# Down projections of a hybrid encoder's gated MLPs, computed on 2x2 blocks by Strassen's algorithm

## The chip, the core and the metric

The kernel runs on one core of a Trainium2 chip. The metric is the device time of one execution in microseconds (us), lower is better. The median of three executions of the kernel before is 1244.37 us (1243.29 to 1244.93).

## The reference, cut to what matters

Everything is float32. Two layers stand one behind the other: a state space mixer (S5) and a differential attention, and behind each a gated MLP, which is what the change touches:

```
def conv_ffn(h, w_up, conv_w, conv_b, w_down):    # h: 512 tokens x 1024; w_up: 1024 x 5632; w_down: 2816 x 1024
    u = h @ w_up
    u = depthwise_conv3_over_tokens(u, conv_w) + conv_b
    g, val = jnp.split(u, 2, axis=-1)             # gate and value, 2816 channels each
    return (jax.nn.silu(g) * val) @ w_down

for i in range(2):
    h = h + mixer_i(rmsnorm(h, norm_mix_g[i]))
    h = h + conv_ffn(rmsnorm(h, norm_ffn_g[i]), ...)
return rmsnorm(h, final_norm_g)
```

## The kernel before, in words

**Split operands.** A product in nearly full float32 precision is made of three faster matmuls. Each operand is split into a high part (ScalarE copies it, rounded, to the type fp32r) and a low part (the value less its high part, one subtraction on VectorE), and `mm3` (lines 801 to 804) adds up high*high, high*low and low*high in PSUM. So each weight and each activation costs one ScalarE and one VectorE instruction per split before TensorE can use it.

**Weights** come as a stream of units (`WStream`, lines 112 to 152): each unit is loaded into one of two raw buffers and split in two halves into one of two pairs of hi and lo buffers. A unit of an up projection (`wup`) has 2048 columns: 8 tiles of 128 input channels by 128 outputs for the gate, and 8 for the value. A unit of a down projection (`wdn`) has 1408: 11 tiles of 128 hidden channels for one tile of 128 outputs.

**The MLP** (`ffn`, lines 909 to 1088) keeps the 512 tokens along the free dimension. The hidden channels are 22 tiles, `j`. Phase by phase: `up(0)` to `up(11)`, `down(0)` over tiles 0 to 10, `up(12)` to `up(21)`, `down(1)` over tiles 11 to 21. An up phase makes, for each `j`, a gate and a value in PSUM (24 matmuls of 512 columns each; "half slot" below). `evac` multiplies them by the norm's factor (`tpb`, VectorE, L927) and starts the convolution (`acc`, ScalarE, L929); half a slot later `conv` adds the other two taps on VectorE (L934, L935), takes silu, multiplies gate by value (L944) and splits the result into `act` (L945 on ScalarE, L946 on VectorE). `later` and `flush` put these a half slot behind. A down phase makes 8 output tiles `m` of 33 matmuls each, and VectorE adds each to the residual `h` (L1005). In the second down phase each finished tile goes through `norm_part`: high part and square on ScalarE, low part on VectorE (L821), the sum of squares on GpSimd (L829). In the last layer six tiles go that way and `finish` makes the last two in halves of 256 tokens.

**What sets the order.** Nothing is scheduled by a planner: every engine executes its instructions in the order in which the program writes them, and waits on semaphores. The matmuls are written ahead of the VectorE and ScalarE work that stands behind them.

Of the kernel before, what the change touches and what calls it, by code (L numbers as in the profile page):

```python
# [9 lines left out]
F32 = mybir.dt.float32  # L10
# [27 lines left out]
def trunk(ctx, tc, xs, xt, sp, bx, cx, sv, vec, lamv, biasw, wglu, wup, wdn, wv, wqk, wo, out):  # L38
# [72 lines left out]

    class WStream:
# [11 lines left out]

        def split(self, half, parts="hl", eng=V):

            i = self.ns
            if i >= len(units):
                return
            n = units[i][1]  # L130
            if half == 0 and "h" in parts:
                self.hl[i] = (
                    self.whl.tile([128, 2048], F32R, tag="hi", name=f"hi{i}"),
                    self.whl.tile([128, 2048], F32R, tag="lo", name=f"lo{i}"),
                )
            h0, h1 = (0, n // 256 * 128) if half == 0 else (n // 256 * 128, n)
            hi, lo = self.hl[i]
            if "h" in parts:
                S.activation(hi[:, h0:h1], self.raw[i][:, h0:h1], AF.Copy)  # L139
            if "l" in parts:  # L140
                eng.tensor_tensor(lo[:, h0:h1], self.raw[i][:, h0:h1], hi[:, h0:h1].bitcast(F32), op=ALU.subtract)  # L141
                if half == 1:
                    del self.raw[i]
                    self.ns += 1

        def start(self):
            self.cur += 1
            while self.nd < min(self.cur + 3, len(units)):
                self.dma()
            return self.hl.pop(self.cur)  # L150

    ws = WStream()
# [571 lines left out]
    ws.whl = pool("whl", 2, "right")  # L724
# [71 lines left out]
    xhi = xnp.tile([128, 8, 512], F32R, name="xhi")  # L796
# [18 lines left out]
    def norm_part(m, gcol, first, split=True):  # L815

        settle()
        if split:
            gc = vect[:, gcol + m:gcol + m + 1]
            S.activation(xhi[:, m], h[:, m], AF.Copy, scale=gc)  # L820
            pend.append(lambda: V.scalar_tensor_tensor(  # L821
                xlo[:, m], h[:, m], gc, xhi[:, m].bitcast(F32), op0=ALU.mult, op1=ALU.subtract))
# [86 lines left out]
    def ffn(l, next_gcol):  # L909
        fp = pool(f"ffn{l}", 1, "left")  # L910
        tpb = [fp.tile([128, 514], F32, name=f"tpb{i}") for i in range(4)]
# [3 lines left out]
        acts = {}  # L915
        state = {"rb": None, "slot": None, "nt": 0}
# [4 lines left out]
        def evac(j, gv, ps):  # L921
            tb = tpb[state["nt"] % 4]
# [5 lines left out]
            acc = fp.tile([128, 512], F32, tag="acc", name="acc", bufs=4)  # L928
# [4 lines left out]
        def conv(j, gv, tb, cw, acc):  # L933
# [7 lines left out]
            if j % 4 == 0:  # L941
                state["slot"] = arena(F32R, [128, 4, 2, 512], f"act{l}_{j}")
            hi, lo = (state["slot"][:, j % 4, i] for i in range(2))
            V.tensor_tensor(a0, a0, acc, op=ALU.mult)  # L944
            S.activation(hi, a0, AF.Copy)  # L945
            later.append(lambda: V.tensor_tensor(lo, a0, hi.bitcast(F32), op=ALU.subtract))  # L946
            acts[j] = (hi, lo)
# [11 lines left out]
        def up(j):  # L959
            w = ws.start()  # L960
            if j == 0:
# [15 lines left out]
                return  # L977
            for gv in range(2):
                ws.split(gv, "h")
                ps = psd[0].tile([128, 512], F32, tag="mm", name="ps", bufs=6)  # L980
                for k in range(8):
                    upmm(w, gv, k, ps)
                    if j == 1 and gv == 0 and k == 5:
# [4 lines left out]
                        evac(0, 1, pss[1])  # L988
                evac(j, gv, ps)
                if j > 1 or gv == 1:  # L990
                    ws.split(gv, "l")

        def down(hf):
            flush()
            for m in range(8 if hf == 0 or l == 0 else 6):
                wh, wl = ws.start()
                if m == 0:
                    flush()
                ws.split(0)
                ws.split(1)  # L1000
                ps = psd[0].tile([128, 512], F32, tag="mm", name="ps", bufs=6)
# [4 lines left out]
                if hf == 1 and l == 0:  # L1006
                    norm_part(m, next_gcol, m == 0)
                elif hf == 1:
                    norm_part(m, next_gcol, m == 0, False)
                    S.activation(hg[:, m], h[:, m], AF.Copy, scale=vect[:, next_gcol + m:next_gcol + m + 1])  # L1010

        def finish():
# [36 lines left out]
            for c in range(2):  # L1049
                cs = slice(256 * c, 256 * c + 256)  # L1050
                for m in (6, 7):
# [7 lines left out]
                    ps = psd[0].tile([128, 512], F32, tag="mm", name="ps", bufs=6)[:, 0:256]  # L1059
                    for k in range(11):  # L1060
                        ah, al = acts[11 + k]
                        mm3(ps, wh[:, k * 128:k * 128 + 128], wl[:, k * 128:k * 128 + 128], ah[:, cs], al[:, cs],
                            k == 0, k == 10)
# [6 lines left out]
                    V.tensor_tensor(h[:, m, cs], ps, h[:, m, cs], op=ALU.add)  # L1070
# [11 lines left out]
        for j in range(12, 22):  # L1082
            up(j)
        down(1)
# [16 lines left out]
    for eh in range(2):  # L1101
        vps = [bank(t, "vps") for t in (("sc", "sc", "sc", "tr"), ("pj", "pj", "pv", "sc"))[eh]]
        for un in range(4):
            wh, wl = ws.start()
            ws.split(0)
            ws.split(1)
            for kl in range(2):
# [289 lines left out]
    fin = pool("fin", 1, "left")  # L1397
    hg = fin.tile([128, 8, 512], F32, name="hg")
# [4 lines left out]
    fin.release()  # L1403
# [108 lines left out]
```

## Time and profile before

| | |
|---|---|
| median of three runs | 1244.37 us |
| the profiled execution | 1244.6 us, its span 1242.8 us |
| TensorE busy | 1178.8 us, 95% of the span |
| VectorE, ScalarE, GpSimd busy | 826.7, 583.3, 253.1 us |
| up phases | 226 to 346, 408 to 520, 873 to 993, 1055 to 1168 us |
| down phases | 346 to 408, 520 to 582, 993 to 1055, 1168 to 1231 us |
| granted TensorE clock, mean | 0.982 |

The span is the time from the first to the last instruction; the execution has 1.8 us around it. An engine's queue works in order, so an instruction that waits holds up all behind it. "Idle before" in a row is the time in which the engine waited ahead of that instruction, and the arrow names what it waited for. Each matmul shows in the rows with a duration that overlaps the next one's; the pace is the distance from start to start.

### The profile page before, as it was taken

Reading aid. Unit: us, or ns where it says so; the run is one execution under the profiler, and the core shown is the slowest. Engines: PE = TensorE matmul, PEld = TensorE weight load, DVE = VectorE, ACT = ScalarE, POOL = GpSimd, SP = SyncE. Lnnn points to the kernel's source line nnn. Section 1 sums busy time; section 2 is a strip of 40 time slices with the busy share of each in tenths; the row PEclk is TensorE's granted clock in tenths of the full one; section 3 lists DMA queues with packets and bytes.
Section 4 is the critical chain, followed back from the end, with each engine's and each line's share of the span. In section 5 each row is a group of like instructions: output and inputs, shape, how many; then the busy total and the mean of one; then the engine's idle time right before and its main releaser. Section 6 shows DMA issues by size and latency. Waiting matters only on the chain.

```text
span 1242.8 us, 16640 instructions
## 1 busy us (share of the span) xinstructions
PE 1178.8 (95%) x6402; PEld 931.5 (75%) x6402; DVE 826.7 (67%) x1654; ACT 583.3 (47%) x1008; POOL 253.1 (20%) x271
## 2 busy tenths in 40 slices
PE   3885999999999999999998999999999999999996
PEld 1663688888878888788876777678888878888786
DVE  8999876667653466745349899977767643566634
ACT  6774654444432344433247777655444421344431
POOL 3999434000000000011033435423000000000011
PEclk8997999999999999999999999999999999999998
DMA  5005322122223222132332323221222233222222
GB/s 219 2 2 136 137 74 102 68 102 102 80 96 114 68 102 102 70 114 71 90 118 83 90 75 104 72 77 63 97 77 94 81 117 125 68 97 75 92 94 68
DMA packets 23391, 112.32 MB, mean 90 GB/s; under 512 B 2704, under 2 KB 5392, under 8 KB 16144
## 3 DMA queue, kind: packets, MB, share of 16 engines
q1 hardware_dynamic: 21472, 108.64, 25.8%
q0 software_dynamic: 1280, 2.10, 0.9%
q8 instruction: 50, 0.82, 0.3%
q10 hardware_dynamic: 560, 0.52, 0.1%
q14 instruction: 29, 0.24, 0.1%
HBM read 102.86 MB, written 2.10 MB: 84 GB/s over the span
## 4 chain that ended last, share of the span: by engine, by line
PE 83%; DVE 13%; ACT 2%; issue 1%; DMA 0%; SPq 0%; DVEq 0%; ACTq 0%
PE ps L803 20%; PE ps L802 20%; PE ps L804 20%; DVE scn L690 2%; PE pj L802 2%; PE pj L804 2%; PE pj L803 2%; DVE St L696 1%; DVE acc L693 1%; PE po L802 1%; PE po L803 1%; PE po L804 1%; PE vps L1112 1%; DVE qkt L1165 1%; PE vps L1114 1%; PE vps L1113 1%
## 5 line engine op out<-in xcount | busy, mean ns | idle before, releaser
L802 PE MATMUL ps<-xhi,hi 128*128 128x512 f32 x672 | 266.9, 397 | 0.0
L803 PE MATMUL ps<-xlo,hi 128*128 128x512 f32 x672 | 265.7, 395 | 0.0
L804 PE MATMUL ps<-xhi,lo 128*128 128x512 f32 x672 | 264.1, 393 | 0.0
L139 ACT ACTIVATE hi<-raw 128x1024 fp32r<-128x1024 f32 (+2 forms) x216 | 184.2, 874 | 113.5 <-PE ps L803 85.8
L141 DVE TENSOR_TENSOR lo<-raw,hi 128x1024 fp32r<-128x1024 f32 (+3 forms) x178 | 188.2, 1076 | 43.5 <-ACT hi L139 41.8
L927 DVE TENSOR_TENSOR tpb<-ps,rb 128x512 f32<-128x512 f32 x88 | 60.8, 692 | 149.9 <-PE ps L804 144.7
L929 ACT ACTIVATE acc<-tpb,vect 128x512 f32<-128x512 f32 x88 | 71.6, 815 | 168.1 <-DVE tpb L927 168.1
L804 PEld LDWEIGHTS ps<-xhi,lo 128*128 128x128 f32 x672 | 126.1, 188 | 31.7
L802 PEld LDWEIGHTS ps<-xhi,hi 128*128 128x128 f32 x672 | 126.2, 188 | 30.7
L803 PEld LDWEIGHTS ps<-xlo,hi 128*128 128x128 f32 x672 | 126.1, 188 | 29.2
L803 PE MATMUL ps<-act,hi 128*128 128x512 f32 (+1 forms) x374 | 144.2, 385 | 0.2
L802 PE MATMUL ps<-act,hi 128*128 128x512 f32 (+1 forms) x374 | 142.8, 382 | 0.0
L804 PE MATMUL ps<-act,lo 128*128 128x512 f32 (+1 forms) x374 | 142.0, 380 | 0.0
L827 POOL COPY ssum<-sqt 128x512 f32<-128x512 f32 x4 | 2.5, 627 | 656.1 <-ACT sqt L824 656.1
L1005 DVE TENSOR_TENSOR h<-ps,h 128x512 f32<-128x512 f32 x30 | 20.7, 690 | 107.4 <-PE ps L804 107.4
L141 POOL TENSOR_TENSOR lo<-raw,hi 128x512 fp32r<-128x512 f32 (+1 forms) x38 | 61.2, 1615 | 119.9 <-ACT hi L139 119.7
L802 PEld LDWEIGHTS ps<-act,hi 128*128 128x128 f32 x374 | 70.3, 188 | 15.9
L804 PEld LDWEIGHTS ps<-act,lo 128*128 128x128 f32 x374 | 70.2, 188 | 15.7 <-DVE lo L141 1.4
L803 PEld LDWEIGHTS ps<-act,hi 128*128 128x128 f32 x374 | 70.3, 188 | 15.3 <-DVE act L946 1.1
L935 DVE SCALAR_TENSOR_TENSOR acc<-tpb,vect,acc 128x512 f32<-128x512 f32 x88 | 66.2, 752 | 3.1
L934 DVE SCALAR_TENSOR_TENSOR acc<-tpb,vect,acc 128x512 f32<-128x512 f32 x88 | 65.4, 743 | 0.6 <-ACT acc L929 0.6
L945 ACT ACTIVATE act<-acc 128x512 fp32r<-128x512 f32 x44 | 27.8, 633 | 66.2 <-DVE acc L944 66.2
(262 smaller groups left out, 2043.5 us busy)
## 6 DMA issues: line engine op xcount, KB each, us to landing
raw<-wup SPq DMA_DIRECT2D x44, 1024.0 KB, 4.8
raw<-wdn SPq DMA_DIRECT2D x32, 704.0 KB, 4.0
raw<-wqk SPq DMA_DIRECT2D x16, 512.0 KB, 3.5
raw<-wglu SPq DMA_DIRECT2D x4, 1024.0 KB, 4.8
raw<-wv SPq DMA_DIRECT2D x8, 512.0 KB, 3.5
raw<-wo SPq DMA_DIRECT2D x4, 1024.0 KB, 4.8
bias<-biasw SPq DMA_DIRECT2D x8, 448.0 KB, 4.1
cxt<-cx SPq DMA_DIRECT2D x1, 2064.0 KB, 15.8
```

Of the source, the lines that this page charges most:

```text
L139: S.activation(hi[:, h0:h1], self.raw[i][:, h0:h1], AF.Copy)
L141: eng.tensor_tensor(lo[:, h0:h1], self.raw[i][:, h0:h1], hi[:, h0:h1].bitcast(F32), op=ALU.subtract)
L690: V.tensor_tensor(prd[dr], st[:, dr].unsqueeze(1).to_broadcast([128, 2, 2, 32]), cft[dr], op=ALU.mult)
L802: PE.matmul(ps, lhsT=wh, rhs=xh, start=first, stop=False)
L803: PE.matmul(ps, lhsT=wh, rhs=xl, start=False, stop=False)
L804: PE.matmul(ps, lhsT=wl, rhs=xh, start=False, stop=last)
L927: V.tensor_tensor(tb[:, 1:513], ps, state["rb"], op=ALU.mult)
L929: S.activation(acc, tb[:, 1:513], AF.Identity, bias=cb, scale=cw[1])
L934: V.scalar_tensor_tensor(acc, tb[:, 0:512], cw[0], acc, op0=ALU.mult, op1=ALU.add)
L935: V.scalar_tensor_tensor(acc, tb[:, 2:514], cw[2], acc, op0=ALU.mult, op1=ALU.add)
L945: S.activation(hi, a0, AF.Copy)
L1005: V.tensor_tensor(h[:, m], ps, h[:, m], op=ALU.add)
```

## The change

Three things change.

**The down projection.** Output tiles are taken in pairs (m, m+1), hidden tiles in five pairs, tokens in two halves of 256. Each is a 2x2 block product, which Strassen's algorithm (Winograd's form, with 7 products and shared sums) computes with 7 block products instead of 8. A block product is 5 hidden pairs of 3 matmuls with 256 columns. The eleventh hidden tile is left over and multiplied as before, in halves. The four sums of weight blocks are made by VectorE (`Pair.total`) ahead of the splits, in the unused part of the raw buffer. VectorE adds six results out of PSUM for each pair (`add`). The weight buffers become 4 pairs of 1024 columns, and the next load is issued right behind the last split of a raw buffer.

**The operands of the tokens.** Seven blocks of 256 tokens for each hidden pair are made in the up phase (`Acts`): `first` splits one block, `second` makes four sums of blocks and splits six. The first three weight operands of a down phase are made within the up slot before it (`early`).

**The norm's low parts** of tiles 2 to 7 at the end of layer 0's MLP are put off into the attention's value projection (`xlows`). `tpb` and `acc` have three buffers instead of four, and `hg` takes the place of `xhi`.

```diff
+    class Pair:                              # the weight operands of two output tiles
+        def total(self, n):
+            w = self.view                    # w(r, odd): raw unit r, even or odd hidden tiles, 5 x 128; w(1): unused part
+            if n == 2:
+                V.tensor_tensor(w(1), w(1, 0), w(1, 1), op=ALU.add)
+            elif n == 3:
+                V.tensor_tensor(w(1), w(1), w(0, 0), op=ALU.subtract)
+            elif n == 4:
+                V.tensor_tensor(w(0, 1), w(0, 1), w(1), op=ALU.subtract)
+            else:
+                self.x = self.ws.xtile()[:, 0:640].rearrange("p (k c) -> p k c", c=128)
+                V.tensor_tensor(self.x, w(0, 0), w(1, 0), op=ALU.subtract)
...
+            S.activation(hi[:, 0:640]..., self.src(n), AF.Copy)                             # h(n)
...
+            V.tensor_tensor(lo[:, 0:640]..., self.src(n), hi[:, 0:640]..., op=ALU.subtract) # l(n)
...
+            def second(self, pa):                                                           # Acts
+                x = ws.xtile().rearrange("p (n c) -> p n c", c=256)
+                b = pa.rearrange("p j (n c) -> p j n c", c=256)
+                S.activation(self.hl[:, 0, 1:3], b[:, 1], AF.Copy)
+                V.tensor_tensor(x[:, 0], b[:, 0, 1], b[:, 0, 0], op=ALU.subtract)
+                V.tensor_tensor(x[:, 1], b[:, 1, 1], b[:, 0, 1], op=ALU.subtract)
+                V.tensor_tensor(x[:, 2], x[:, 1], b[:, 0, 0], op=ALU.add)
+                V.tensor_tensor(x[:, 3], b[:, 1, 0], x[:, 2], op=ALU.subtract)
+                S.activation(self.hl[:, 0, 3:7], x, AF.Copy)
+                V.tensor_tensor(self.hl[:, 1, 1:3], b[:, 1], self.hl[:, 0, 1:3].bitcast(F32), op=ALU.subtract)
+                later.append(lambda: V.tensor_tensor(self.hl[:, 1, 3:7], x, self.hl[:, 0, 3:7].bitcast(F32),
+                                                     op=ALU.subtract))
...
+                if early and gv == 0:                                                       # up
+                    ws.split(0, "l")
+                    ws.split(1)
+                elif early:
+                    w = ws.hl[ws.cur + 1]
+                    w.total(2)
+                    w.h(2)
+                    w.l(2)
+                    w.total(3)
                 evac(j, gv, ps)
...
         def down(hf):
-            flush()
-            for m in range(8 if hf == 0 or l == 0 else 6):
...
-                for k in range(11):
-                    ah, al = acts[hf * 11 + k]
-                    mm3(ps, wh[:, k * 128:k * 128 + 128], wl[:, k * 128:k * 128 + 128], ah, al, k == 0, k == 10)
-                V.tensor_tensor(h[:, m], ps, h[:, m], op=ALU.add)
...
+                def prod(n, op, name, part=0, first=False):
...
+                    for kp in range(5):
+                        mm2(bank[name][:, half[part]], hi[:, 128 * kp:128 * kp + 128], lo[:, 128 * kp:128 * kp + 128],
+                            *acts[hf, kp].op(op), first and kp == 0)
...
+                prod(0, 0, "b1", 0, True)
+                if prev:
+                    prev()                   # last add of the pair before, and its norm
+                if mp > 0:
+                    w.l(2)
+                    w.total(3)
+                w.h(3)
+                flush()
+                prod(1, 1, "b2", 0, True)
+                add(h[:, m, half[0]], bank["b1"][:, half[0]])
+                w.total(4)
+                w.h(4)
+                w.l(3)
+                prod(2, 3, "b5", 0, True)
+                w.h(5)
+                w.l(4)
+                w.total(6)
+                w.done(0)                    # frees a raw buffer: the next load is issued
+                flush()
+                prod(3, 5, "b1")
+                add(h[:, m:m + 2, half[1]], twice(bank["b5"][:, half[0]]))
+                w.h(6)
+                w.l(5)
+                w.done(1)
+                prod(4, 2, "b2", 1)
+                left(4, "b2")
+                add(h[:, m, half[1]], bank["b1"][:, half[0]])
+                w.l(6)
+                ws.split(0, "h")
+                flush()
+                prod(5, 6, "b4", 0, True)
+                left(5, "b4")
+                add(h[:, m], bank["b2"])
+                norm(m)
+                ws.split(0, "l")
+                ws.split(1, "h")
+                prod(6, 4, "b1")
+                add(h[:, m + 1], bank["b4"])
+                ws.split(1, "l")             # and total(2), h(2) of the next pair
```

On VectorE, where the first up phase ends and the first down phase begins, there stood before (L946 is a low part of `act`, L1005 the first output tile's addition to `h`):

```order
L946 TENSOR_TENSOR act_8_3295<-acc,act_8_3295 128x512
L934 SCALAR_TENSOR_TENSOR acc<-tpb_2585,vect,acc 128x512
L935 SCALAR_TENSOR_TENSOR acc<-tpb_2585,vect,acc 128x512
L141 TENSOR_TENSOR lo_3408<-raw_3333,hi_3407 128x768
L934 SCALAR_TENSOR_TENSOR acc<-tpb_2586,vect,acc 128x512
L935 SCALAR_TENSOR_TENSOR acc<-tpb_2586,vect,acc 128x512
L944 TENSOR_TENSOR acc<-acc 128x512
L946 TENSOR_TENSOR act_8_3295<-acc,act_8_3295 128x512
L141 TENSOR_TENSOR lo_3485<-raw_3405,hi_3484 128x640
L141 TENSOR_TENSOR lo_3485<-raw_3405,hi_3484 128x768
L1005 TENSOR_TENSOR h<-ps,h 128x512
```

At the same place now (L156 and L158 are the weight sums 3 and 4, L174 a weight's low part, L1026 and L1027 the taps of the convolution, L1178 an addition to `h`; the last row is the low part of weight operand 3):

```order
L174 TENSOR_TENSOR lo<-raw_3476,hi 128x640
L156 TENSOR_TENSOR raw_3476<-raw_3476,raw_3396 128x640
L1019 TENSOR_TENSOR tpb_2597<-ps,rb 128x512
L1039 TENSOR_TENSOR act_0_1_2918<-acc,act_0_0_2761 128x512
L1026 SCALAR_TENSOR_TENSOR acc<-tpb_2596,vect,acc 128x512
L1027 SCALAR_TENSOR_TENSOR acc<-tpb_2596,vect,acc 128x512
L1026 SCALAR_TENSOR_TENSOR acc<-tpb_2597,vect,acc 128x512
L1027 SCALAR_TENSOR_TENSOR acc<-tpb_2597,vect,acc 128x512
L1046 TENSOR_TENSOR pa<-acc 128x512
L1178 TENSOR_TENSOR h<-ps,h 128x256
L158 TENSOR_TENSOR raw_3396<-raw_3396,raw_3476 128x5x128
L174 TENSOR_TENSOR lo<-raw_3476,hi 128x640
```

The weight sums and splits now stand between and behind the gate work of the last slot, and the low part that the fourth block product reads is the last row shown.

On TensorE the first output tile of that down phase began before with rows of this kind, eleven hidden tiles of three:

```order
L802 MATMUL ps<-act_0_2718,hi_3407 128x512
L803 MATMUL ps<-act_0_2718,hi_3407 128x512
L804 MATMUL ps<-act_0_2718,lo_3408 128x512
L802 MATMUL ps<-act_0_2718,hi_3407 128x512
L803 MATMUL ps<-act_0_2718,hi_3407 128x512
L804 MATMUL ps<-act_0_2718,lo_3408 128x512
```

And now with a block product of five hidden pairs (`fifth` holds the operands of the fifth pair):

```order
L1150 MATMUL ps<-act_0_0_2761,hi 128x256 x2
L1150 MATMUL ps<-act_0_0_2761,lo 128x256
L1150 MATMUL ps<-act_0_1_2918,hi 128x256 x2
L1150 MATMUL ps<-act_0_1_2918,lo 128x256
L1150 MATMUL ps<-act_0_2_3075,hi 128x256 x2
L1150 MATMUL ps<-act_0_2_3075,lo 128x256
L1150 MATMUL ps<-act_0_3_3232,hi 128x256 x2
L1150 MATMUL ps<-act_0_3_3232,lo 128x256
L1150 MATMUL ps<-fifth,hi 128x256 x2
L1150 MATMUL ps<-fifth,lo 128x256
```

The matmuls are half as wide, and seven such products with twelve left-over matmuls stand where two tiles of 33 stood.

## Rows read from the trace of the kernel before

**Rows 1.** The page: span and busy time by engine (busy us, share, instructions).

```profile
span 1242.8 us, 16640 instructions
PE 1178.8 (95%) x6402; PEld 931.5 (75%) x6402; DVE 826.7 (67%) x1654; ACT 583.3 (47%) x1008; POOL 253.1 (20%) x271
```

**Rows 2.** Busy us (and instructions) by engine in the first up phase and down phase.

```profile
226.00:346.00 120.00, 120.00 (x521) 96.69 (x520) 82.76 (x108) 53.66 (x68) 0.00 (x0) 1.00 0.24 83
...
346.00:408.00 62.00, 62.00 (x266) 49.59 (x265) 24.72 (x33) 14.44 (x20) 0.00 (x0) 1.00 0.36 121
```

**Rows 3.** TensorE's matmuls where 512 columns give way to 256 (start, duration).

```profile
1179.76 0.39 PE L802 MATMUL ps<-act,hi 128*128 128x512 f32 x1
...
1213.36 0.28 PE L802 MATMUL ps<-act,hi 128*128 128x256 f32 x1
...
1219.60 0.28 PE L803 MATMUL ps<-act,hi 128*128 128x256 f32 x1
```

**Rows 4.** VectorE in order of time, from up phase to down phase at 520 us.

```profile
511.45 1.22 DVE L141 TENSOR_TENSOR lo<-raw,hi 128x1024 fp32r<-128x1024 f32 x1
...
519.99 0.69 DVE L927 TENSOR_TENSOR tpb<-ps,rb 128x512 f32<-128x512 f32 x1 [1.93 <-PE ps L804]
520.60 0.68 DVE L946 TENSOR_TENSOR act<-acc,act 128x512 fp32r<-128x512 f32 x1
521.20 0.75 DVE L934 SCALAR_TENSOR_TENSOR acc<-tpb,vect,acc 128x512 f32<-128x512 f32 x1
...
522.65 0.95 DVE L141 TENSOR_TENSOR lo<-raw,hi 128x768 fp32r<-128x768 f32 x1
523.52 0.74 DVE L934 SCALAR_TENSOR_TENSOR acc<-tpb,vect,acc 128x512 f32<-128x512 f32 x1
...
525.15 0.69 DVE L944 TENSOR_TENSOR acc<-acc 128x512 f32<-128x512 f32 x1
...
527.18 1.70 DVE L141 TENSOR_TENSOR lo<-raw,hi 128x640 fp32r<-128x640 f32 x2
528.79 0.68 DVE L1005 TENSOR_TENSOR h<-ps,h 128x512 f32<-128x512 f32 x1
```

**Rows 5.** VectorE, all steps of 256 elements: strided, contiguous, out of PSUM.

```profile
L773 DVE TENSOR_TENSOR gx<-tr,gx 128x256 fp32r<-128x256 f32 x14 | 5.9, 424 | 1.8 <-ACT gx L772 1.4
...
1217.89 0.41 DVE L1070 TENSOR_TENSOR h<-ps,h 128x256 f32<-128x256 f32 x1
...
1228.97 1.74 DVE L1045 TENSOR_TENSOR hg<-hg,rp 128x256 f32<-128x256 f32 x5 [2.22 <-ACT rb L1038]
1230.63 0.47 DVE L1041 SCALAR_TENSOR_TENSOR hg<-h,vect,rp 128x256 f32<-128x256 f32 x1
```

**Rows 6.** ScalarE's high parts and taps; then the loads of `wdn` (KB, us to landing).

```profile
512.11 0.73 ACT L139 ACTIVATE hi<-raw 128x640 fp32r<-128x640 f32 x1
515.12 0.82 ACT L929 ACTIVATE acc<-tpb,vect 128x512 f32<-128x512 f32 x1 [2.29 <-DVE tpb L927]
...
raw<-wdn SPq DMA_DIRECT2D x32, 704.0 KB, 4.0
```

**Rows 7.** TensorE after its longest wait in the attention, then the granted clock there.

```profile
786.51 1.09 PE L1266 MATMUL ptp<-ident,s 128*128 128x128 f32 x4 [2.92 <-DVE s L1256]
...
788.25 0.63 PE L804 MATMUL po<-o,lo 128*128 128x512 f32 x1
788.68 0.63 PE L802 MATMUL po<-o,hi 128*128 128x512 f32 x1
...
788.00:789.00 1.00, 1.00 (x4) 0.81 (x3) 0.86 (x4) 1.00 (x3) 0.00 (x0) 0.50 0.97 410
789.00:790.00 1.00, 1.00 (x5) 0.77 (x5) 1.00 (x2) 1.00 (x3) 0.00 (x0) 0.86 0.89 377
```

**Rows 8.** GpSimd's sum and VectorE's two low parts beside it, second down phase.

```profile
537.88 1.30 POOL L829 TENSOR_TENSOR ssum<-ssum,sqt 128x512 f32<-128x512 f32 x1 [6.39 <-ACT sqt L824]
...
538.39 2.33 DVE L141 TENSOR_TENSOR lo<-raw,hi 128x640 fp32r<-128x640 f32 x2 [1.28 <-ACT hi L139]
```

More of the change, by code (lines that the diff above doesn't have):

```diff
@@ L123, in dma, with tiles @@
                 self.nd += 1
+        def tiles(self):
+            return [self.whl.tile([128, 1024], F32R, tag=t, name=t) for t in ("hi", "lo")]
         def split(self, half, parts="hl", eng=V):
@@ L130, in split @@
             n = units[i][1]
+            pair = i in pair_at
             if half == 0 and "h" in parts:
[L132 to L135, printed above, removed]
+                self.hl[i] = Pair(self, i) if pair else (Cols(), Cols())
+            if pair:
+                for c in parts:
+                    (self.hl[i].h if c == "h" else self.hl[i].l)(half)
+                if half == 1 and "l" in parts:
+                    self.ns += 2
+                return
             h0, h1 = (0, n // 256 * 128) if half == 0 else (n // 256 * 128, n)
@@ L138, in split @@
             if "h" in parts:
+                if half == 0 or n > 1024:
+                    for c, t in zip((hi, lo), self.tiles()):
+                        c.parts.append((t, h0, h1 if n > 1024 else n))
                 S.activation(hi[:, h0:h1], self.raw[i][:, h0:h1], AF.Copy)
@@ L813, in settle, with norm_part @@
         pend.clear()
-    def norm_part(m, gcol, first, split=True):
+    xlows = {}
+    def norm_part(m, gcol, first, split=True, put=None):
         settle()
@@ L909, in ffn @@
     def ffn(l, next_gcol):
+        hg = None
         fp = pool(f"ffn{l}", 1, "left")
-        tpb = [fp.tile([128, 514], F32, name=f"tpb{i}") for i in range(4)]
+        tpb = [fp.tile([128, 514], F32, name=f"tpb{i}") for i in range(3)]
         for t in tpb:
@@ L915, in ffn @@
         acts = {}
+        fifth = [None]
+        ws.xtile = lambda: fp.tile([128, 1024], F32, tag="x", name="x", bufs=1)
         state = {"rb": None, "slot": None, "nt": 0}
@@ L940, in conv @@
             a0 = state["gate"]
[L941 to L947, printed above, removed]
+            hf, jl = j // 11, j % 11
+            if jl == 10:
+                hi, lo = acts[hf, "left"] = [acts[hf, i].rest for i in range(2)]
+                V.tensor_tensor(a0, a0, acc, op=ALU.mult)
+                S.activation(hi, a0, AF.Copy)
+                later.append(lambda: V.tensor_tensor(lo, a0, hi.bitcast(F32), op=ALU.subtract))
+                return
@@ new lines, in conv @@
+            kp = jl // 2
+            if jl % 2 == 0:
+                state["pa"] = fp.tile([128, 2, 512], F32, tag="pa", name="pa", bufs=1)
+                state["pair"] = Acts(hf, kp)
+            pa, ab = state["pa"], state["pair"]
+            V.tensor_tensor(pa[:, jl % 2], a0, acc, op=ALU.mult)
+            wait = hf == 1 and kp == 0
+            if wait and jl % 2 == 1:
+                later.append(lambda: (ab.first(pa), later.append(lambda: ab.second(pa))))
+            elif not wait:
+                later.append(lambda: (ab.first if jl % 2 == 0 else ab.second)(pa))
@@ L977, in up @@
                 return
+            early = ws.ns in pair_at
             for gv in range(2):
-                ws.split(gv, "h")
+                if early and gv == 1:
+                    pass
+                else:
+                    ws.split(gv, "h")
                 ps = psd[0].tile([128, 512], F32, tag="mm", name="ps", bufs=6)
@@ L988, in up, with mm2 @@
                         evac(0, 1, pss[1])
+                if early and gv == 0:
[7 more added lines that the diff above has]
+                    w.total(3)
                 evac(j, gv, ps)
-                if j > 1 or gv == 1:
+                if not early and (j > 1 or gv == 1):
                     ws.split(gv, "l")
+        def mm2(ps, wh, wl, ah, al, first):
+            for i, (w, x) in enumerate(((wh, ah), (wh, al), (wl, ah))):
+                PE.matmul(ps, lhsT=w, rhs=x, start=first and i == 0, stop=True, skip_group_check=True)
@@ L993, in down @@
         def down(hf):
[L994 to L1010 removed]
+            npair = 4 if hf == 0 or l == 0 else 3
```

146 lines of the change are left out of this document (128 added, 18 removed).

## The prediction

> **What bounds the kernel now.** I began with the page: TensorE is busy for 95% of the span, VectorE for 67% [rows 1]. An average over stages says nothing about one stage, so next I read busy time by stretch. In an up phase TensorE is busy for 120.00 of 120.00 us and VectorE for 82.76; in the first down phase TensorE for 62.00 of 62.00 and VectorE for only 24.72 [rows 2]. So the stretches that the change touches are TensorE's, and VectorE has much room in the down phase, less in the up phase. Then I read TensorE's matmuls one by one for their pace, and VectorE's queue in order of time where up turns into down, because the change gives VectorE far more to do just there.
>
> **What TensorE saves.** The pace is read where 512 columns give way to 256 [rows 3]: 144 matmuls from 1179.76 to 1213.36 make 0.2333 us each, 52 from there to 1219.60 make 0.120 each. Half as wide is a little more than half as long. A pair of output tiles was 2 x 33 = 66 matmuls of 512: 15.40 us. It becomes 7 products of 15 matmuls and 12 left-over ones, 117 of 256: 14.04 us. There are 4 + 4 + 4 + 3 = 15 pairs; the last two tiles keep their count. 15 x 1.36 = 20.4 us saved, if nothing waits.
>
> The Trainium skill prices this otherwise ("TensorE: Matmul & The Clock Gate", section Back-to-back issue gap: columns by 2.4 GHz and 2.5 ns more). By that, as an estimate, 216 and 109 ns, so 15 x (14.24 - 12.78) = 21.9 us. The rows differ by 18 and 11 ns a matmul, and I take the rows.
>
> **What VectorE gets, by the piece.** I charge each instruction the distance from its start to the next one's start. From [rows 4]: `tpb` 0.61 (519.99 to 520.60), a low part of 512 elements 0.60, the two taps of a convolution 1.45 (521.20 to 522.65), or 1.63 if the product of gate and value follows (523.52 to 525.15) and with that product 2.24, two low parts of 640 together 1.61 (so 0.80), one of 1024 1.14 (its 1.22 less the same overlap). 256 elements take 0.33 in a row [rows 5], 0.45 if each needs the one before, 0.38 as an `add` out of PSUM. No row shows a sum of 5 x 128 elements at a stride of 256. The nearest is a strided 256 at 424 ns, against 0.41 contiguous [rows 5], so I charge 0.80 as for a plain 640, and 0.85 where the next step needs it. The bounds are half of that and twice it.
>
> **The pairs, once running.** Per pair: seven low parts of 640 (5.6) with two of 128 (0.5), four sums (3.2), four adds of 512 and two of 256 (3.2): 12.5 us beside 14.04 of TensorE. It fits, and I walked through the order for due times. The tightest is weight operand 3: VectorE reaches it some 0.3 us before product 3 needs it. Loads are no limit: a raw buffer is freed 8.6 us before the next pair begins, and a `wdn` load lands after 4.0 [rows 6]. I charge nothing here, and up to 1 us a pair if the sums are dearer.
>
> **The up phase.** Per two hidden tiles, two low parts of 512 (1.2) become low parts of 256, 512 and 1024 and four sums (0.33 + 0.60 + 1.14 + 1.80 = 3.87). The worst half slot is now `tpb` 0.61, sums 1.80, low part 0.60, taps 1.45, weight split 1.14: 5.60. It starts 0.2 after a half slot ends, and what it splits is due 0.47 into the half slot that follows the next 5.6. So it is done at 5.8 and due at 6.07. The half slots beside it need less. No charge; with dearer sums some 0.2 us on 20 such half slots.
>
> **The seam, where up turns into down.** Before, TensorE ran through it without a wait. Now the last up slot of VectorE carries the first three weight operands, and behind it the gate work, and only then comes what product 3 needs. Count from the first matmul of the last up unit; half slots end at 5.6 and 11.2, products are due at 11.2, 13.0, 14.8 and 16.6, and product 3 reads its weight's low part first in its third matmul, at 16.84.
>
> Seam of the first down phase in each layer. VectorE comes free at 5.8, from the worst half slot. Then, in the order of the queue: low parts 0 and 1 (1.60), `tpb` (0.61), a low part of 1024 (1.14), taps and product (2.24), sum 2 (0.85), a wait for ScalarE's high part of it (0.73 by [rows 6] and two hand-overs, 0.83), low part 2 (0.85), sum 3 (0.82), `tpb` (0.61), left-over low part (0.60), taps (1.45), taps and product (2.24), add (0.38), sum 4 (0.85), low part 3 (0.80). That is 15.9, so 21.7 against 16.84: TensorE waits 4.8 us. Behind product 3 stand all other matmuls.
>
> Seam of the second down phase. VectorE comes free of its half slot at 5.05 (`tpb` to 0.8, ScalarE's taps 0.82 [rows 6] and a high part of 256 at about half a 640's, low part 0.38, taps 1.45, split 1.14), and follows with low parts 0 and 1 behind ScalarE (to 6.9), `tpb`, taps and product (9.75), sum 2, wait, low part 2, sum 3 (13.1), `tpb` (13.7), four sums (15.5), low part of 512 (16.1). Product 1 needs that one for its fifth pair at 14.56: 1.5 late. Taps (17.55), low part of 1024 (18.7), which product 2 needs at 17.9: 0.8 late. Taps and product (20.95), add, sum 4, low part 3: 23.0, where product 3, already late, needed it at 19.2: 3.8 more. Together 6.1.
>
> Two of each: 2 x 4.8 + 2 x 6.1 = 21.8 us.
>
> **The clock behind a wait.** In the attention TensorE once waited 2.92 us; after it the granted clock stood at 0.50 until within the slice from 789, and 512 columns went at 0.43 instead of 0.2333 [rows 7]. From 786.5 to some 789.3 at half rate, 1.4 us of work were lost. Each seam has a single wait of 3.8 us or more, longer than that one, so I charge 4 x 1.4 = 5.6.
>
> **The norm beside the pairs.** In the second down phases GpSimd adds up squares. A pair of low parts beside such a sum took 2.33 us, against 1.70 alone [rows 8, 4]: 0.6 lost. With 0.3 of slack this costs 0.3 to 0.6 on the five borders between pairs there, a postponed low part once more: 2 us.
>
> The Trainium skill ("SBUF — State Buffer", section Who interferes with whom) speaks of an exclusive lock between GpSimd and a VectorE instruction with two inputs from SBUF. By that the loss could be GpSimd's whole 1.30 a time and the term 5 instead of 2; the row shows half of it, since the low part came in the middle.
>
> The rest costs nothing: the postponed low parts of layer 0 (6 x 0.78) stand in the value projection, whose units give VectorE 5.6 us each for two splits of 512; the halved weight buffers change no due time, and the loads, issued a little earlier, share SyncE's queue only with the attention's bias tables, which are fetched a head ahead.
>
> **The sum** is made against the profiled execution, 1244.6, which is 0.2 above the median: -20.4 + 21.8 + 5.6 + 2.0 = +9.0, so 1253.6 us. The sum is a small difference between two larger numbers, and the second is the less certain.
>
> **Rivals.**
> - *The saving shows (faster).* The mechanism: VectorE's seam queue is shorter than I count, because narrow or strided sums cost less than rows of plain work say. At half price the sums save 1.3 in the first seam and 1.8 in the second, which leaves 3.5 and 4.3 and a time near 1247, so this alone does not turn the sign. It does from 3 us a seam with no fall of the clock: -20.4 + 12 + 2 = -6.4, so 1238. With no seam at all it is 1224.2. For it: TensorE ran these borders without a wait. Against it: the queue is fixed, and most of the 15.9 us are rows of before.
> - *Seams as counted, the clock stays up.* The waits are cut by single matmuls with high parts. Then +3.4 with the norm's 2: 1248. Against it: [rows 7].
> - *VectorE binds throughout.* At twice the price, four sums add 3.3 us to each pair: 15.8 against 14.04, 15 x 1.8 = 27 us beyond the saving, and every half slot with sums slips by 1. Against it: [rows 5]. Time 1270 to 1285.
>
> **How the numbers follow.** Forecast 0.58 (1250 to 1260 by itself), clock stays up 0.14 (1245 to 1250), VectorE binds 0.11, saving shows 0.17 (1224 to 1244). About 0.2%, 2.5 us, is what a measurement of this kernel can tell from no change. From these: faster 0.15, same 0.08, slower 0.77. The range 1239 to 1268 leaves out the far ends of the first and the last rival.
>
> **What would show it.** Right: TensorE's rows in a down phase at a pace of 0.120; at each of the four borders a wait of 3.5 to 5 us before the third matmul of product 3, released by VectorE's low part; a clock of 0.50 for some 3 us behind it; no such wait later in a first down phase. Wrong: TensorE busy through the borders, or waits that recur in every pair, or in every second hidden tile of an up phase. The forecast falls if the four waits come to less than 15 us together.

## The result, and the profile after

The changed kernel takes 1265.63 us (median of four runs, 1264.49 to 1265.92) against 1244.65 us for the kernel before (four runs on the same chip, 1243.29 to 1245.97). The ratio is 1.0162, with a 95% interval of 1.0149 to 1.0175. So it is 21 us slower, where 9 were forecast: the sign was right, and the size forecast was less than half of the measured one. The profiled execution took 1264.49 us, its span 1262.7 us against 1242.8 [rows 1].

The first lines of the page. TensorE has less to do, VectorE much more: 991.1 us instead of 826.7.

```profile
span 1262.7 us, 18725 instructions
PE 1174.3 (93%) x7167; PEld 965.7 (76%) x7167; DVE 991.1 (78%) x1953; ACT 632.0 (50%) x1103; POOL 254.7 (20%) x269
```

What TensorE waited for, from the list of waits (us in total, times, longest). Before, it waited for none of these in the MLPs.

```profile
PE ps L1150 <- DVE h L1178: 10.9, 4, 3.3
PE ps L1150 <- DVE lo L174: 7.4, 12, 1.2
PE vps L1362 <- DVE h L1178: 1.4, 1, 1.4
PE ps L1150 <- DVE fifth L1085: 1.1, 2, 0.5
PE ps L1150 <- ACT fifth L1078: 1.0, 2, 0.5
PE ps L887 <- DVE lo L222: 0.9, 4, 0.3
```

L1178 is `add`, L174 a weight's low part (`Pair.l`), L222 the same in an up phase. The four waits for `add` are the four borders; but the low parts are waited for twelve times, four of them at the borders, and the forecast knew of no others.

**The first seam.** TensorE's rows at the border into the first down phase of layer 0, and VectorE's queue beside them (start, duration; in brackets the idle time before).

```profile
352.30 0.28 PE L1150 MATMUL ps<-fifth,lo 128*128 128x256 f32 x1
355.86 0.47 PE L1150 MATMUL ps<-act,hi 128*128 128x256 f32 x2 [3.28 <-DVE h L1178]
357.24 0.58 PE L1150 MATMUL ps<-act,lo 128*128 128x256 f32 x1 [0.91 <-DVE lo L174]
```

```profile
353.83 0.75 DVE L1027 SCALAR_TENSOR_TENSOR acc<-tpb,vect,acc 128x512 f32<-128x512 f32 x1
354.69 0.69 DVE L1046 TENSOR_TENSOR pa<-acc 128x512 f32<-128x512 f32 x1
355.30 0.42 DVE L1178 TENSOR_TENSOR h<-ps,h 128x256 f32<-128x256 f32 x1
355.63 0.81 DVE L158 TENSOR_TENSOR raw<-raw,raw 128x640 f32<-128x640 f32 x1
356.36 1.79 DVE L174 TENSOR_TENSOR lo<-raw,hi 128x640 fp32r<-128x640 f32 x2
```

Product 3 adds to the bank out of which `add` must first read; `add` stands behind taps and product of the last gate work. Against the pace of 0.120, the distances from 352.30 on come to 4.8 us lost, as in the sum. The clock falls behind it, as after the attention's wait [rows 7]; the column behind POOL is the granted clock (0.50 is the lower of its two levels, 1.2 of 2.4 GHz; a matmul of 256 columns then takes 0.213 us from start to start, from 357.62 to 359.97):

```profile
356.00:357.00 1.00, 0.33 (x2) 0.13 (x2) 1.00 (x2) 0.44 (x1) 0.00 (x0) 0.95 0.00 0
357.00:358.00 1.00, 0.76 (x3) 0.76 (x4) 0.85 (x2) 1.00 (x3) 0.00 (x0) 0.50 0.00 0
359.00:360.00 1.00, 1.00 (x7) 1.00 (x7) 1.00 (x3) 0.74 (x1) 0.00 (x0) 0.50 0.00 0
360.00:361.00 1.00, 1.00 (x9) 1.00 (x9) 1.00 (x4) 0.00 (x0) 0.00 (x0) 0.84 0.85 163
```

**Later pairs.** What was not forecast. ScalarE in the first and in the second down phase of layer 0, where a next pair's high parts are due; then GpSimd's sum and VectorE's sum 4 beside it; then TensorE one pair later, where the next such sum 4 (from 564.33) lasted 1.58.

```profile
394.14 1.37 ACT L168 ACTIVATE hi<-raw 128x640 fp32r<-128x640 f32 x2 [4.80 <-DMA raw<-wdn]
...
572.96 0.74 ACT L168 ACTIVATE hi<-raw 128x640 fp32r<-128x640 f32 x1 [3.54 <-DMA raw<-wdn]
573.60 0.71 ACT L905 ACTIVATE xhi<-h,vect 128x512 fp32r<-128x512 f32 x1
574.21 0.61 ACT L913 ACTIVATE sqt<-h 128x512 f32<-128x512 f32 x1
574.74 0.72 ACT L168 ACTIVATE hi<-raw 128x640 fp32r<-128x640 f32 x1
```

```profile
547.38 1.89 POOL L918 TENSOR_TENSOR ssum<-ssum,sqt 128x512 f32<-128x512 f32 x1 [3.82 <-ACT sqt L913]
```

```profile
548.35 1.59 DVE L158 TENSOR_TENSOR raw<-raw,raw 128x640 f32<-128x640 f32 x1
```

```profile
566.70 0.39 PE L1150 MATMUL ps<-act,lo 128*128 128x256 f32 x1 [1.22 <-DVE lo L174]
```

ScalarE stands still for 3.5 to 4.8 us because the weights have not landed, and then the norm's two instructions come between the two high parts. Sum 4 (L158), 0.81 elsewhere, lasts 1.59 beside GpSimd. Busy time in that phase (TensorE, its weight loads, VectorE, ScalarE, GpSimd; clock): VectorE's 32.13 of 62 us in the same phase before (first row) have become 56.69 of 65 (second row).

```profile
520.00:582.00 62.00, 61.90 (x266) 49.41 (x265) 32.13 (x39) 21.38 (x33) 8.40 (x7) 1.00 0.28 96
...
526.00:591.00 65.00, 57.45 (x449) 55.23 (x448) 56.69 (x87) 31.94 (x54) 8.90 (x7) 0.97 0.25 84
```

**Where the 19.9 us of the span went**, from the starts of the phases in both traces:

| stretch | forecast | measured |
|---|---|---|
| up to the first down phase, S5 above all (same code) | 0 | +1.05 |
| first down phases, layers 0 and 1 | +0.8, +0.8 | +1.85, +0.98 |
| second up phases, both | 0 | +2.0 |
| second down phase, layer 0 (61.96 to 69.24) | +3.1 | +7.28 |
| second down phase, layer 1 (46.56 to 52.30) | +4.4 | +5.74 |
| finish | 0 | +0.9 |

The rest, 0.1, is in the attention.

### The profile page after: what moved, and what is told of

It reads as the page before. It is cut to its first block, busy times and chain, and to the rows that moved or that the text cites. A ratio compares the mean times of both kernels' runs of the same rounds, so it can differ in the third digit from the quotient of the medians.

```text
span 1262.7 us, 18725 instructions
## 1 busy us (share of the span) xinstructions
PE 1174.3 (93%) x7167; PEld 965.7 (76%) x7167; DVE 991.1 (78%) x1953; ACT 632.0 (50%) x1103; POOL 254.7 (20%) x269
## 4 chain that ended last, share of the span: by engine, by line
PE 69%; DVE 21%; ACT 4%; DMA 2%; issue 2%; ACTq 0%; SPq 0%; DVEq 0%
PE ps L887 12%; PE ps L885 12%; PE ps L886 12%; PE ps L1150 9%; DVE lo L174 2%; PE pj L885 2%; PE pj L887 2%; PE pj L886 2%; DVE scn L773 1%; ACT hi L168 1%; PE po L885 1%; PE po L886 1%; PE vps L1362 1%; DMA raw<-wdn 1%; PE po L887 1%
## 5 line engine op out<-in xcount | busy, mean ns | idle before, releaser
L1150 PE MATMUL ps<-act,hi 128*128 128x256 f32 x1016 | 194.1, 289 | 11.7 <-DVE h L1178 10.9
L1150 PEld LDWEIGHTS ps<-act,hi 128*128 128x128 f32 x1016 | 161.0, 194 | 13.3 <-issue 11.6
L220 ACT ACTIVATE hi<-raw 128x1024 fp32r<-128x1024 f32 (+2 forms) x156 | 140.0, 910 | 32.2 <-DMA raw<-wv 10.4
L1150 PE MATMUL ps<-act,lo 128*128 128x256 f32 x508 | 147.3, 290 | 7.5 <-DVE lo L174 7.4
L222 DVE TENSOR_TENSOR lo<-raw,hi 128x1024 fp32r<-128x1024 f32 (+2 forms) x118 | 134.3, 1147 | 23.5 <-ACT hi L220 21.8
L168 ACT ACTIVATE hi<-raw 128x640 fp32r<-128x640 f32 x90 | 64.9, 732 | 98.7 <-DMA raw<-wdn 38.5
L1150 PEld LDWEIGHTS ps<-act,lo 128*128 128x128 f32 x508 | 99.1, 195 | 10.7 <-DVE lo L174 10.7
L174 DVE TENSOR_TENSOR lo<-raw,hi 128x640 fp32r<-128x640 f32 x90 | 74.9, 836 | 23.8 <-ACT hi L168 22.5
L222 POOL TENSOR_TENSOR lo<-raw,hi 128x512 fp32r<-128x512 f32 (+1 forms) x38 | 61.2, 1616 | 120.9 <-ACT hi L220 120.8
L1027 DVE SCALAR_TENSOR_TENSOR acc<-tpb,vect,acc 128x512 f32<-128x512 f32 x88 | 66.2, 752 | 3.1
L1026 DVE SCALAR_TENSOR_TENSOR acc<-tpb,vect,acc 128x512 f32<-128x512 f32 x88 | 65.6, 745 | 0.6 <-ACT acc L1021 0.6
L1178 DVE TENSOR_TENSOR h<-ps,h 128x256 f32<-128x256 f32 (+1 forms) x90 | 53.6, 596 | 9.4 <-PE ps L1150 9.4
L918 POOL TENSOR_TENSOR ssum<-ssum,sqt 128x512 f32<-128x512 f32 x26 | 38.9, 1494 | 95.4 <-ACT sqt L913 95.2
```

What stands on the lines that cost most here:

```text
L168: S.activation(hi[:, 0:640].rearrange("p (k c) -> p k c", c=128), self.src(n), AF.Copy)
L174: V.tensor_tensor(lo[:, 0:640].rearrange("p (k c) -> p k c", c=128), self.src(n), hi[:, 0:640].bitcast(F32).rearrange("p (k c) -> p k c", ...
L1026: V.scalar_tensor_tensor(acc, tb[:, 0:512], cw[0], acc, op0=ALU.mult, op1=ALU.add)
L1027: V.scalar_tensor_tensor(acc, tb[:, 2:514], cw[2], acc, op0=ALU.mult, op1=ALU.add)
L1150: PE.matmul(ps, lhsT=w, rhs=x, start=first and i == 0, stop=True, skip_group_check=True)
```

## Experiments

Ratios are to the kernel before, run on the same chip; the changed kernel stands at 1.0162, and 0.001 is 1.25 us.

**e1_seam: the gate work behind the add.** In the last up slot `evac` is held back, and `down` calls it further on.

```
 up, early:  w.total(3)
+            gate = later.pop(); flush(); flush(); later.append(gate)
+            state["held"] = lambda ps=ps: evac(j, 1, ps)
 down:       w.h(3)
-            flush()
             prod(1, ...); add(...); w.total(4); w.h(4); w.l(3)
+            if mp == 0: state["held"]()
```

> The changed kernel; only the order of VectorE's work at the four borders into a down phase differs: the last gate work of the up phase (its tpb, the convolutions, the product) is written behind the first add, total(4) and l(3) of the first pair, instead of ahead of them. Theory 1 (order: TensorE waits there because the add out of b1 and the low parts stand behind gate work in VectorE's queue): the waits of 4.8 and 6.1 us fall below 2 us each, the granted clock stays at 1.0 behind them, and the time goes from 1265.6 to 1240 to 1250. Theory 2 (capacity: VectorE has 11.9 us of its own work in a pair of 14.0 us, and 4 to 5 us of gate work do not fit, in whatever order): the waits come back at products 4 to 6 or in the second pair, and the time is 1255 to 1263.

Measured: 1264.09 us, 1.0152 (1.0137 to 1.0167). Theory 1 falls; the waits come back as theory 2 says, but the time is 1 us above its range. The waits for `add` are gone, and the low parts have taken their place (7.4 us before):

```profile
PE ps L1156 <- DVE lo L174: 15.7, 22, 1.8
PE ps L1156 <- ACT act L1038: 2.6, 2, 1.3
```

In the first down phase of layer 0 the clock now stays at 1.00 around its waits, but the phase lasts 64.41 us instead of 63.66, for the pairs behind start late as well. VectorE had no time left in the first pair, busy for 4.86 of 5.00 us:

```profile
357.00:362.00 5.00, 3.25 (x28) 3.04 (x27) 4.86 (x10) 0.74 (x1) 0.00 (x0) 1.00 0.30 88
```

**e2_half: loads of half the size.** It leaves out 640 of the 1408 columns of each unit.

```
+                n = 768 if n == 1408 and i in halves else n
-                SY.dma_start(out=r[:, 0:n], in_=src)
+                SY.dma_start(out=r[:, 0:n], in_=src[:, 0:n])
```

> The changed kernel with shorter loads: each weight load of a pair brings 768 of its 1408 columns (384 KB instead of 704), and the operands of odd hidden tiles are read from the columns of the even ones, so that the weights used are wrong; instruction counts and sizes stay. Theory 1 (loads: the 9 us lost in pairs two to four come from loads that land late, ScalarE waiting 3 to 5 us for them): the loads land in 2.5 to 3.2 us, these losses fall to 3 us or less, and the time is 1257 to 1261. Theory 2 (they come from VectorE's own queue and from GpSimd's lock): 1264 to 1266.

Measured: 1258.61 us, 1.0109 (1.0093 to 1.0126): 6.6 us less, theory 1 by the time, though the loads land in 3.6 us and not in 2.5 to 3.2, and the later pairs and the border still lose 5.1 us in its trace and not 3. The edit also takes the stride out of the reads of the weights; that changes no duration (0.82 us for sum 2 either way). The profiled execution was the slowest of the four (1261.94 us), so its trace shows less of the gain than the times. Its loads in the first down phase of layer 0 (KB, median us to landing; 5.5 us for 704 KB in the changed kernel there), and TensorE's waits for low parts, 7.4 us before:

```profile
raw<-wdn SPq DMA_DIRECT2D x6, 384.0 KB, 3.6
```

```profile
PE ps L1153 <- DVE lo L176: 5.4, 9, 0.9
```

**e3_nosum: without GpSimd's sums.**

```
-        else:
+        elif add:                      # False in the second down phases
             G.tensor_tensor(ssum[0], ssum[0], sqt, op=ALU.add)
```

> The changed kernel without GpSimd's sums of squares in the two second down phases (the norms behind them use the first tile's squares alone). Theory 1 (lock: two VectorE instructions of a pair last 1.45 to 1.59 instead of 0.81 us beside such a sum, and VectorE's low parts then come late): the later pairs of the second down phases lose 2 to 3 us instead of 7.0, and the time is 1260 to 1263. Theory 2 (late loads set those waits): within 1 us of 1265.6, the waits of ScalarE for the loads unchanged.

Measured: 1259.92 us, 1.0109 (1.0091 to 1.0127): 6.6 us less, though ScalarE waits for loads nearly as long as before (34.9 instead of 38.5 us). Sum 4 is back at 0.81, and the waits of a later pair fall:

```profile
580.44 0.81 DVE L158 TENSOR_TENSOR raw<-raw,raw 128x640 f32<-128x640 f32 x1
```

```profile
582.04 0.39 PE L1150 MATMUL ps<-act,lo 128*128 128x256 f32 x1 [0.45 <-DVE lo L174]
```

So either cure, shorter loads or no lock, takes most of the same loss away. They are two parts of one shortage: VectorE comes late and has no slack to catch up.

**e8_raw3: a third raw buffer**, in half of `xlo`, for units 2 and 5 of each second down phase. Nothing is left out; this is the test of the loads by themselves.

```
+    if i in spare: r = xnp.tile([128, 2048], F32, tag="xl1", ...)
+    ws.dma()                           # ahead of down(1)
```

> The changed kernel with one edit alone: the third raw buffer of m4_raw3 in the second down phases. Theory 1 (loads: 4 to 5 of the 7.0 us that the later pairs of these phases lose stem from loads that land late): 1259.5 to 1262, ScalarE's waits there gone. Theory 2 (the lock and VectorE's queue alone): 1263.5 to 1266.

Measured: 1261.42 us, 1.0127 (1.0113 to 1.0140): 4.4 us less, theory 1. In the second down phase of layer 0 the waits behind the first pair fall from 0.27, 1.22, 0.29 and 1.21 us to 0.27, 0.16 and 0.16. ScalarE's waits for loads (38.5 us before) and TensorE's for low parts, then one of the pairs:

```profile
ACT hi L170 <- DMA raw<-wdn: 20.6, 6, 3.9
...
PE ps L1166 <- DVE lo L176: 4.8, 12, 0.9
```

```profile
565.84 0.38 PE L1166 MATMUL ps<-act,lo 128*128 128x256 f32 x1 [0.16 <-DVE lo L176]
```

**m2: the gate work spread.** In the first down phases the last slot's gate work, which makes a hidden tile of the second half and is not needed there, goes to the end of the first and of the second pair. In the second ones the left-over products of the first pair stand at the pair's end. The norm stands behind the next pair's high parts.

```
 down:  prod(1, ...); add(...); w.total(4); w.h(4); w.l(3)
+       if mp == 0: state["held"]()    # tpb and the middle tap only
 ...
        w.l(6)
+       step()                         # one piece of gate work
 ...
+       if spread: left(4, "b2"); left(5, "b4"); add(h[:, m], bank["b2"]); norm(m)   # behind prod(6)
```

> Like e1_seam, and more: the gate work of the last slot is spread over the first pair (in the first down phases over the first two pairs), the left-over tile's products of the first pair of the second down phases stand at the pair's end, and the norm's instructions of a tile stand behind ScalarE's high parts of the next pair instead of ahead. Theory 1 (order): no wait over 1.5 us at the four borders, the clock at 1.0 there, 1236 to 1244 us, at or below the kernel before. Theory 2 (capacity): 1250 to 1260.

Measured: 1254.55 us, 1.0084 (1.0064 to 1.0105), by the time in the range of theory 2. The trace divides it: the first down phases last 58.65 and 58.29 us instead of 63.66 and 62.78, so there the spread work fits. The second one of layer 0 lasts 69.87, no shorter than 69.24: there the work is needed within the pair.

**m4_raw3 and m5_raw3_nosum: m2 with the third raw buffer, then without sums as well.** The edits are those of e8_raw3 and e3_nosum.

> m2 with a third raw buffer in the second down phases (in half of xlo, which is free there), so that the first load of a pair is issued a step earlier. Theory 1 (late loads hold ScalarE's high parts and so VectorE's low parts): ScalarE's waits for these loads of 3 to 5 us vanish, the pairs lose 4 to 5 us less in the two phases together, 1248 to 1251. Theory 2 (VectorE is full there: 11.9 us and two instructions that the lock makes 0.8 us longer, of 14.0 us): ScalarE waits for VectorE instead, 1253 to 1256.

> m4_raw3 without GpSimd's sums of squares in the second down phases (the norms behind use the first tile's squares alone). Theory 1 (capacity): two VectorE instructions of each pair go back from 1.5 to 0.81 us, VectorE catches up, and the time is 4 to 7 us below m4_raw3, 1242 to 1247. Theory 2 (what is left there is the chain of high part, low part and product, not VectorE's time): within 2 us of m4_raw3.

Measured: 1249.12 us, 1.0028 (1.0017 to 1.0038), and 1246.65 us, 1.0002 (0.9989 to 1.0014). The buffer is worth 7 us to m2, theory 1. Behind it the lock is worth 3.2, below the 4 to 7 of theory 1 and above the 2 of theory 2. Both kernels still lose 4.9 us in the first pair of each second down phase, and neither beats the kernel before.

**m3_firstonly: block products in the first down phases alone**, the second ones as before.

```
-    pair_at = {4 + o + m for o in (12, 30) for m in (0, 2, 4, 6)} | ...
+    pair_at = {u + 12 + m for u in (4, f1) for m in (0, 2, 4, 6)}
-        down(1)
+        down1(1)                       # the loop of the kernel before
```

> The block products in the first down phase of each layer alone, with the gate work spread as in m2; the second down phases, their operands and the finish are those of the kernel before. Theory 1 (capacity: a pair's 11.9 us of VectorE work fit into 14.0 us where nothing else is due, and do not where the norm stands beside them): first down phases of 58 to 59 us instead of 61.8, all else as before, so 1244.6 less 6.6, 1236 to 1241. Theory 2 (the operands made in the up phases and the border cost what the products save): 1243 to 1248.

Measured: 1244.21 us, 0.9988 (0.9978 to 0.9999), by the time in the range of theory 2. The first down phases took 61.29 and 58.04 us against 61.81 and 61.80: in layer 0 a load came late again (0.38 us of waiting for a high part at 377.13, then some 0.4 us in each pair), and the attention's first matmul waited 0.88 us for the last `add`. The load behind the wait at 377.13 was issued at 370.07 and took 6.2 us.

**m9_border and m6.** m9 lays another PSUM bank where the MLP's last one is; m6 also moves sum 6 up, which frees a raw buffer earlier.

```
+    bank("aux", "aux")                 # m9, m6 and m7: ahead of the value projection
 mp > 0: w.l(2); w.total(3)
+        w.total(6)                     # m6 and m7
```

> m6 without the early total(6), that is m3_firstonly with the bank edit alone. Theory 1 (the border into the attention is worth 1.0 us and the earlier loads in the first down phases 1 to 2 us): 1242.5 to 1244, above m6. Theory 2 (the earlier total(6) delays low part 3 as much as it advances the loads): 1240.5 to 1242, as m6.

> m3_firstonly with two edits: total(6) of pairs two to four stands right behind total(3), so that a raw buffer comes free 0.8 us earlier, and another bank of PSUM is put where the last bank of the MLP lies, so that the attention's first matmul waits for no add of the MLP. Theory 1 (in m3 the gain of the first down phase of layer 0 went to late loads, 3.3 us, and 1.0 us to the border into the attention): no wait at that border, first down phases of 58 to 59.5 us, 1238 to 1242. Theory 2 (m3's missing gain is scatter of the S5 stage, and the loads stay late): 1242 to 1245.

Measured: m9 1242.41 us, 0.9974 (0.9962 to 0.9985); m6 1241.34 us, 0.9960 (0.9947 to 0.9973). The wait at the border into the attention is gone in m6, whose first down phases last 59.29 and 58.69 us; TensorE waits for low parts four times there, for 2.9 us in all, no less than the changed kernel in the same two phases (four times, 2.3); what is gone are the waits of 3.3 us for `add`:

```profile
PE ps L1178 <- DVE lo L173: 2.9, 4, 0.9
PE ps L1178 <- DVE h L1206: 0.4, 2, 0.2
```

m6 is faster than both kernels. m9 lies between its two theories, and m6's step over it is not sure, for the two intervals overlap.

**m7: the same two edits on m4_raw3.**

> m4_raw3 with the two edits of m6. Theory 1 (the border costs 1.2 us there, and a buffer that is free 0.8 us earlier takes 1 to 2 us of VectorE's late low parts): 1245.5 to 1247.5. Theory 2 (VectorE's time in the second down phases is what is left, 4 to 5 us at each border and the lock): 1247.5 to 1250.

Measured: 1252.40 us, 1.0055 (1.0041 to 1.0069): slower than m4_raw3, by neither theory. The border's wait is gone, but in the second down phases sum 6 (L163) now delays `add` and low part 3 (L176, doubled by a GpSimd sum beside it):

```profile
542.61 0.82 DVE L163 TENSOR_TENSOR x<-raw,raw 128x640 f32<-128x640 f32 x1
543.34 0.75 DVE L923 SCALAR_TENSOR_TENSOR xlo<-h,vect,xhi 128x512 fp32r<-128x512 f32 x1
544.00 0.42 DVE L1205 TENSOR_TENSOR h<-ps,h 128x256 f32<-128x256 f32 x1
544.34 0.82 DVE L160 TENSOR_TENSOR raw<-raw,raw 128x640 f32<-128x640 f32 x1
545.07 2.63 DVE L176 TENSOR_TENSOR lo<-raw,hi 128x640 fp32r<-128x640 f32 x2
```

```profile
544.57 0.47 PE L1177 MATMUL ps<-act,hi 128*128 128x256 f32 x2 [0.86 <-DVE h L1205]
547.01 0.38 PE L1177 MATMUL ps<-act,lo 128*128 128x256 f32 x1 [1.98 <-DVE lo L176]
```

## Why the prediction was right in sign and short in size

*What TensorE saves* was right. With 0.120 us a matmul the 15 pairs fill 210.6 us of the four down phases, which took 232.1 before: 21.5 saved, 20.4 forecast. In the later pairs three matmuls take 0.359 us from start to start, so 0.120 each.

*The seam* was right, 21.1 us in the four together against 21.8: 4.84 and 4.82 at the first ones, 5.7 at each of the second ones, there in the three places that were reckoned (some 1.4, 0.8 and 3.5, against 1.5, 0.8 and 3.8). VectorE's queue ran as worked out to within 0.3 us. One detail was off: TensorE stops twice in product 3, first for `add` and then in the third matmul for the low part.

*The clock behind a wait* was about right in size: the first pairs of the four phases lost 27.6 us against the pace of 0.120, 6.5 more than the seams themselves, with the granted clock at 0.50 behind each seam, against 5.6. In part that was luck. The charge rested on a single wait of 3.8 us at each seam; the longest were 3.28 at the first ones and 2.17 at the second ones, which is shorter than the attention's 2.92, and the clock fell all the same.

*The pairs, once running* was the step that failed: "Loads are no limit: a raw buffer is freed 8.6 us before the next pair begins, and a `wdn` load lands after 4.0 [rows 6]. I charge nothing here". In the third pair of layer 0 the buffer came free at 388.48, when sum 6 ended, 6.6 us before the next pair began at 395.09, and ScalarE had the weights at 394.14, 5.7 us later. High and low part need another 1.6, so nothing was left. Three things made the difference. The due time itself was too early: in pairs that lost nothing (the second of layer 0, pairs two to four of e2_half's first down phases) sum 6 ended 6.86 us behind the pair's first matmul, where 8.6 before the next one means 5.4. Of the two loads of a pair, now issued 1.5 us apart, where before they came one by one (4.0 [rows 6]), the first took 3.8 to 4.2 in eleven of twelve cases (here 5.5), but the second mostly 5.3 to 6.2. And sum 2 of the next pair needs the second one, so VectorE began the third pair late and reached its sum 6 at 7.4:

```profile
381.36 0.83 DVE L154 TENSOR_TENSOR raw<-raw 128x640 f32<-128x640 f32 x1 [0.32 <-DMA raw<-wdn]
```

With the next, the later pairs and the border into the attention cost 9.7 us where 2.0 were charged: 1.5 and nothing in the two first down phases, 6.1 and 2.2 in the second ones. The 8.3 of these two are 3.6 with the third buffer (e8_raw3), 2.0 without the sums (e3_nosum) and 5.1 with short loads (e2_half), the border included, by the starts of the pairs in the traces.

*The norm beside the pairs* failed in the same way. It was charged 0.6 a time, less the slack. In layer 0 sum 4 lost 0.78 each time and a low part 0.64, in layer 1 sum 3 lost 0.98: seven instructions, 5.5 us. That the 0.3 of slack had already gone to the loads is argued, not shown. Without the sums the kernel gains 6.6 us (e3_nosum). The Trainium skill ("SBUF — State Buffer", section Who interferes with whom) says that the port pair which the two engines share is an exclusive lock, that a VectorE instruction with two SBUF inputs contends for it with a GpSimd instruction that reads SBUF, and that the order of issue decides who blocks. Here the trace agrees: GpSimd's sum ran from 547.38 to 549.27, and sum 4, begun at 548.35, ended at 549.94, 0.67 behind it. The rule that the prediction weighed and discounted for a row with a late overlap was the better guide, though one time cost 0.78 here and not the whole 1.30.

*No charge* for the up phases, the border into the attention and the finish was wrong by 2.0, 1.6 and 0.9 us. Each is a low part or an `add` that is late by 0.2 to 1.5 us. The 1.05 us ahead of the MLP lie in code that did not change; over the profiled kernels of this study the first down phase began between 344.30 and 348.22 us. In all the forecast missed 10.9 us of the span: 6.8 in the down phases (later pairs and border 7.7, clock 0.9, less 0.7 at the seams and 1.1 that TensorE saved beyond the sum) and 4.0 outside them.

*The rivals.* "VectorE binds throughout" has the place of the loss nearly right and its cause wrong: the sums cost 0.82 us and not twice 0.80, and the waits recur in every pair, one of the prediction's signs of being wrong, only where the norm stands beside them. In the first rival the sums at half price save 2.2 us in the second seam, by the terms of the seam, and not 1.8; its time near 1247 stays.

*The deeper fault* is one of method. The sum priced VectorE by due times within a pair that starts on time. A pair that begins on time runs at TensorE's pace with VectorE busy for 11.84 of 13.99 us (the second pair of layer 0). But 12.5 of 14.04 us leave 1.5 for everything else, and late loads, lock, norm and gate work each want a part of it. e1_seam shows it best: put in another order, the same work cost the same. It could be taken away only where it is not needed soon (m2's first down phases, 4 to 5 us each) or where its causes go (m4_raw3, m5_raw3_nosum). Seams, clock and later pairs (21.1, 6.5 and 9.7) are counted row by row and make up the 37.4 us, but for rounding, that the four phases lost; how the 9.7 divide between loads that are issued late, second loads that take longer and the lock stays open, for each cure takes part of the others' share, and why a first load once took 5.5 us no run shows.

## What to carry to other kernels

When work moves from a full engine to one with room, add up the second engine's time for each stretch with all that stands beside it (norms, locks, left-over work), and at some 85% (11.9 of 14.0 us a pair, 56.7 of 65 in a second down phase) count on no room: the pairs ran at pace while nothing was late, but a late load is not caught up there, and another order of the same work gained nothing. Make the exchange only in the stretches where the room is real: here the two first down phases, which alone, with the gate work spread and the two edits of m6, make the kernel 0.4% faster than before, while all four make it 1.6% slower as first written and still 0.3% with the gate work spread and a third buffer (m4_raw3).

## What was not expected of the hardware

- A wait of 1.75 us for a low part left the granted clock at 1.00 (e1_seam, from 359.03). So did waits of 1.29 and 0.89 close together (from 537.24). In the same kernel a wait of 1.60 and one of 0.35 close together, from 1026, were followed by 0.73 and 0.61 of full speed (rows below), so the length of the waits alone does not tell:

```profile
1029.00:1031.00 2.00, 2.00 (x14) 1.87 (x13) 2.00 (x4) 1.15 (x2) 0.00 (x0) 0.73 0.00 0
1031.00:1034.00 3.00, 2.89 (x16) 2.73 (x16) 2.85 (x6) 2.10 (x5) 0.00 (x0) 0.61 0.01 3
```

- Of two loads of 704 KB issued 1.5 us apart, the second landed after 5.3 to 6.2 us in nine of ten cases (once 4.5); issued 2.1 apart, after 4.4 and 4.5. Single ones took 4.0 [rows 6], and so did most of the first ones.
- Sums of 5 x 128 elements at a stride of 256 (L154, 0.82 us) cost VectorE no more than a low part that is read without a stride (L174, 0.81 to 0.83): the price taken, not its bounds.
